# First 256 columns of x loaded as two times 128, with the first weight slab's rows between them, and the first feature tile multiplied ahead of the second's transposes

## The chip, the cores and the metric

The kernel runs on one core of a Trainium2 chip. The metric is device time in microseconds; the time of the kernel before is the median of three runs.

## The reference

One layer of a decoder trunk on x of 512 tokens by 2048 features, in float32:

```
h    = RMSNorm(x)
proj = h @ w_in                     # 2048 x 4608: q, k, v of two head groups
x    = x + concat(norm(stick_breaking(q, k, v)), norm(sliding_window(q, k, v))) @ w_out
h    = RMSNorm(x)
x    = x + (silu(gate) * up) @ w_down,   gate, up = split(h @ w_gate_up)
out  = RMSNorm(x)
```

The change lies in the first microseconds: the loading and transposing of x, and the first of the input projections, the values of the first head group (512 of w_in's columns at a time).

## The kernel before, in words

Every float32 product is done as three products of a cheaper format: an operand is split into a high part (rounded to fp32r by ScalarE, `hi`) and the rest (`lo`, by VectorE), and PE adds hi x hi, hi x lo and lo x hi in the same PSUM bank. So each operand costs one ScalarE and one VectorE instruction before PE can use it.

**The start.** x comes as four token tiles (128 tokens each) by column pieces `XC`, the first 256 columns wide. `load_x(0)` issues the four transfers of the first piece, `load(0)` two transfers of 128x512 of the first weight slab (one for each of its two rows of 128 features), `load_x(1)` the next four of x, `load(1)` slab 1 as one transfer of 512 KB. All go through SP's queue in program order (`dma` keeps it), and every transfer carries one of eight semaphores in turn, so that SP issues a transfer only when the one eight places ahead of it has landed. An issue can thus wait for a landing.

**Feature tiles.** `h_make(kt)` makes one feature tile of h: PE transposes the four token tiles' columns into a PSUM bank `z` (128 features by 512 tokens), ScalarE makes `hhi` of it, scaled by the norm's gain, VectorE `hlo` (`split_scaled`). The transposes are issued through `pT`, which pins them to program order; so are the matmuls of `warm(n)`, which multiply a constant `ones` into an unused bank, each showing as two instructions on PE. `split_scaled` itself is not pinned.

**Slabs.** A slab is 256 of the 2048 features of w_in by 512 columns; `queue` holds the slabs and, for each, 8 steps (`mms`): two feature tiles by four token tiles, three products each. `step()` does one: at a slab's step 0 it calls `split(i)` (if not done yet), at step 2 it loads the two slabs ahead and calls `split(i + 1)`, which for the first eight slabs first makes that slab's two feature tiles with `h_make`, then `whi` and `wlo` of the whole slab (128x1024). For slab 0 `split` goes by rows: `h_make(0)`, `whi` and `wlo` of row 0, then the same for row 1, with `pA` and `pV`, which pin. For later slabs they go through `A` and `V`, which do not. Where an instruction isn't pinned, the framework's scheduler places it in its engine's order when the program is built. The chip then runs each engine's list as it stands.

`x_squares` (row sums of squares of x for the norm, in place on ScalarE) are deferred to the last of these slabs in the program, and are put by the scheduler wherever ScalarE seems free.

Of the kernel before, what the change touches and what calls it, by code (L numbers as in the profile page):

```python
# [16 lines left out]
P = 128  # L17
# [20 lines left out]
def tile_hymba(ctx: ExitStack, tc: tile.TileContext, x, ln_mix, w_in, sb_norm, swa_norm,  # L38
               sinks, w_out, ln_ffn, w_gu, w_dn, ln_fin, out):
    nc = tc.nc  # L40
    x2d = x.rearrange("b s d -> (b s) d")
# [24 lines left out]
    def act8(name, dt=F32R):  # L66
        return act.tile([P, 4, 512], dt, tag="a8", name=name, bufs=8)
# [7 lines left out]
    def pz():  # L75
        return zs[1].tile([P, 512], F32, tag="z", name="z", bufs=4)
# [17 lines left out]
    def tmp(dt=F32, name="t"):  # L94
        return phase[1].tile([P, 512], dt, tag="t", name=name, bufs=phase[2])
# [3 lines left out]
    def dma(out, in_):  # L99
        tc.keep_in_program_order(nc.sync.dma_start(out=out, in_=in_))  # L100

    def f(ap):
        return ap.bitcast(F32)
# [49 lines left out]
    def warm(n):  # L153
        for _ in range(n):
            pT.matmul(busy[:, 0:P], lhsT=ones, rhs=ones, start=True, stop=True)
# [23 lines left out]
    def load(i):  # L179
        sl = queue[i]  # L180
        if "raw" in sl:
            return
        a, b, srcs = sl["a"], sl["b"], sl["srcs"]
        if sl["big"] is not None:

            if not sl["big"]:
                sl["big"].append(big_pool[0].tile([P, 2 * a, b], F32, tag="raw8", name="raw8", bufs=2))
                dma(out=sl["big"][0], in_=srcs[0].rearrange("(a p) c -> p a c", p=P))
                sl["raw"] = sl["big"][0][:, 0:a, :]
            else:  # L190
                sl["raw"] = sl["big"][0][:, a:2 * a, :]
            return
        raw = wp.tile([P, a, b], F32, tag="raw", name="raw", bufs=RAWB)
        n = b // len(srcs)
        if i == 0:
            for j in range(a):
                dma(out=raw[:, j, :], in_=srcs[0][j * P:(j + 1) * P, :])
            srcs = []
        for k, src in enumerate(srcs):
            dma(out=raw[:, :, k * n:(k + 1) * n], in_=src.rearrange("(a p) c -> p a c", p=P))  # L200
        sl["raw"] = raw

    def split(i):
        sl = queue[i]
        if "hi" in sl:
            return
        load(i)
        if sl["prep"] and i:
            sl["prep"]()
        a, b, raw = sl["a"], sl["b"], sl["raw"]  # L210
        hi = wp.tile([P, a, b], F32R, tag="whi", name="whi", bufs=2)
        lo = wp.tile([P, a, b], F32R, tag="wlo", name="wlo", bufs=2)
        if i == 0:
            for j in range(a):
                h_make(j)
                pA.activation(out=hi[:, j, :], in_=raw[:, j, :], func=AF.Copy)
                pV.tensor_tensor(out=lo[:, j, :], in0=raw[:, j, :], in1=f(hi)[:, j, :], op=ALU.subtract)
        else:
            A.activation(out=hi, in_=raw, func=AF.Copy)  # L219
            V.tensor_tensor(out=lo, in0=raw, in1=f(hi), op=ALU.subtract)  # L220
        sl["hi"], sl["lo"] = hi, lo
# [4 lines left out]
    def step():  # L226

        i, m = pos
        sl = queue[i]
        if m == 0:  # L230
            split(i)
            if sl["pre"]:
                sl["pre"]()
        if m == min(2, len(sl["mms"]) - 1):
            for k in (1, 2):
                if i + k < len(queue):
                    load(i + k)
            if i + 1 < len(queue):
                split(i + 1)
        t = sl["mms"][m](sl["hi"], sl["lo"])  # L240
        pos[1] += 1
        if pos[1] == len(sl["mms"]):
            pos[0] += 1
            pos[1] = 0
            if sl["post"]:
                sl["post"]()
        for d in list(due):
            d[0] -= 1
            if d[0] <= 0:
                due.remove(d)  # L250
                d[1]()
        return t

    def pull(ns, mark=None):

        mark = len(queue) if mark is None else mark
        carry[0] += ns
        while carry[0] > 0 and pos[0] < mark:
            carry[0] -= step()
# [4 lines left out]
    def drain(mark=None):  # L264

        mark = len(queue) if mark is None else mark
        while pos[0] < mark:
            step()

    def split_scaled(ps_ap, g_ap, hi, lo):  # L270
        A.activation(out=hi, in_=ps_ap, func=AF.Copy, scale=g_ap)
        V.scalar_tensor_tensor(out=lo, in0=ps_ap, scalar=g_ap, in1=f(hi), op0=ALU.mult, op1=ALU.subtract)
# [35 lines left out]
    XC = [(0, 256), (256, 256), (512, 512), (1024, 512), (1536, 512)]  # L308
    ss1 = const.tile([P, NT, len(XC)], F32, name="ss1")
    xs = {}  # L310
    rs1 = {}

    def load_x(c):
        c0, n = XC[c]
        for t in range(NT):
            xt = tmp(name="xt")[:, 0:n]
            dma(out=xt, in_=x2d[t * P:(t + 1) * P, c0:c0 + n])
            for k in range(n // P):
                xs[c0 // P + k, t] = xt[:, k * P:(k + 1) * P]
            xs["c", c, t] = xt  # L320

    def h_make(kt):
        pb = pz()
        for t in range(NT):
            pT.transpose(out=pb[:, t * P:(t + 1) * P], in_=xs[kt, t], identity=ident)
            warm({(0, 0): 1, (0, 1): 1, (0, 2): 3, (1, 3): 3}.get((kt, t), 0))
        if kt % 4 == 0:
            h8[0], h8[1] = act8("hhi"), act8("hlo")
        h_hi[kt], h_lo[kt] = h8[0][:, kt % 4, :], h8[1][:, kt % 4, :]
        split_scaled(pb, gcol[:, kt:kt + 1], h_hi[kt], h_lo[kt])  # L330
# [112 lines left out]
    def add_v(c):  # L443
        def v_done(t, pb):
            bv = pb.rearrange("p (h d) -> p h d", d=HD)
            split_scaled(bv, rs1["c"][:, t:t + 1], vst[t][:, c * 8:(c + 1) * 8, 0:HD],
                         vst[t][:, c * 8:(c + 1) * 8, HD:P])

        def prep(s):
            if c == 0:  # L450
                h_make(2 * s)
                h_make(2 * s + 1)
                if s == 7:
                    defer(1, lambda: [x_squares(k) for k in range(3)])
                    defer(2, lambda: [x_squares(k) for k in range(3, 5)])
                    defer(4, rstd1_make)
                    defer(8, rstd1_rows)
        add_tok(lambda s: win[s * 256:(s + 1) * 256, C_SBV + c * 512:C_SBV + (c + 1) * 512],
                8, 2, 512, hT, lambda: four(1 - c), v_done, prep)
# [11 lines left out]
    add_v(0)  # L471
    add_v(1)
    load_x(0)
    load(0)
    turn1()
    load_x(1)
    load(1)
    load_x(2)
    for c in (3, 4):
        while pos[0] < c - 3 or pos[1] < 3:  # L480
            step()
        load_x(c)
# [1176 lines left out]
```

## Time and profile before

| | us |
|---|---|
| median of 3 runs | 2019.59 (2019.31 to 2021.86) |
| the profiled execution's own time | 2019.78 |
| its span | 2017.7 |
| PE busy | 2004.0 |
| VectorE busy, ScalarE busy, GpSimd busy | 1454.5, 1455.9, 1030.7 |
| first product of the projection on PE (start) | 8.40 |
| first product of slab 1 on PE (start) | 14.95 |

The span is the stretch that the profiler saw, from the program's first instruction to its last; the time of an execution has 2.1 us around it. A row of the timeline gives start, length, engine, line, operation and tiles (out<-in, without numbers), the count of merged instructions, and in brackets the engine's idle time before it and what ended that. PE rows are pipelined: their lengths overlap, and start to start is what one costs. L118 is the line of the helper through which all pinned instructions go; L358 to L360 are there the three products of `one` in `add_tok`.

### The profile page before, as it was taken

The page shows a single profiled execution, that of the slowest core. Times are in us where ns is not written, and L with a number is a line of the kernel's source. Part 1 is how long each engine was busy: PE and PEld are TensorE (multiplying, and loading weights), DVE is VectorE, ACT ScalarE, POOL GpSimd, SP SyncE. Part 2 cuts the span into 40 slices and gives each one's busy share as a digit, 9 for nine tenths or more (in the row PEclk, how much of TensorE's full clock was granted, in tenths as well). Part 3 has the DMA queues.
Part 4 walks back from the last instruction along what each step waited for, and adds up shares of the span by engine and source line. Part 5 has one row for each costly group of instructions (what it writes and reads, how often), then busy time and mean ns, then how long its engine had stood idle before and what let it go on. Part 6 is the DMA issues. An engine that isn't in the chain of part 4 may idle for free.

```text
span 2017.7 us, 29248 instructions
## 1 busy us (share of the span) xinstructions
PE 2004.0 (99%) x10412; PEld 1708.3 (85%) x10412; DVE 1454.5 (72%) x1968; ACT 1455.9 (72%) x2009; POOL 1030.7 (51%) x562
## 2 busy tenths in 40 slices
PE   9999999999999999999999999999999999999998
PEld 8888888898888888888888888888888888888886
DVE  4358888778963777777777777777777867767767
ACT  5347777657842478777777777777777788788787
POOL 0014444300100066766666676666766778878883
PEclk9999999999999999999999999999999999999999
DMA  5322222222343354453544535444453743533523
GB/s 189 94 84 74 63 63 71 66 75 73 105 146 110 118 165 115 121 135 101 141 110 126 133 103 142 107 129 128 108 141 105 263 160 109 180 129 105 176 84 115
DMA packets 286369, 240.23 MB, mean 119 GB/s; under 512 B 11024, under 2 KB 237392, under 8 KB 283792
## 3 DMA queue, kind: packets, MB, share of 16 engines
q1 hardware_dynamic: 285552, 235.71, 39.5%
q8 instruction: 82, 1.34, 0.3%
q0 software_dynamic: 288, 1.32, 0.2%
q10 hardware_dynamic: 384, 1.34, 0.2%
q14 instruction: 63, 0.52, 0.1%
HBM read 218.40 MB, written 19.92 MB: 118 GB/s over the span
## 4 chain that ended last, share of the span: by engine, by line
PE 97%; DVE 1%; ACT 1%; issue 0%; DVEq 0%; POOL 0%; ACTq 0%; POOLq 0%
PE o L118 34%; PE m L118 28%; PE m L390 4%; PE m L391 4%; PE m L392 4%; PE m L359 2%; PE m L358 2%; PE m L360 2%; PE o L359 2%; PE o L360 2%; PE o L358 2%; PE z L118 1%; PE z L358 1%; PE z L359 1%; PE z L360 1%; PE o L685 1%
## 5 line engine op out<-in xcount | busy, mean ns | idle before, releaser
L118 POOL TENSOR_TENSOR t<-raw,t 128x1024 f32<-128x1024 f32 x107 | 272.6, 2548 | 278.0 <-ACT hp L118 263.7
L118 DVE TENSOR_TENSOR wlo<-t,hp 128x1024 fp32r<-128x1024 f32 x235 | 286.4, 1219 | 172.6 <-PE o L118 107.2
L118 ACT ACTIVATE whi<-t 128x1024 fp32r<-128x1024 f32 x235 | 249.2, 1061 | 123.7 <-PE o L118 75.3
L118 PE MATMUL o<-hca,whi 128*128 128x512 f32 x880 | 307.5, 391 | 0.0
L118 POOL TENSOR_TENSOR t<-raw,raw 128x1024 f32<-128x1024 f32 x106 | 275.1, 2599 | 16.6 <-issue 10.9
L118 DVE TENSOR_TENSOR wlo<-raw,hp 128x1024 fp32r<-128x1024 f32 x175 | 213.5, 1220 | 80.0 <-issue 49.8
L118 ACT ACTIVATE whi<-raw 128x1024 fp32r<-128x1024 f32 (+1 forms) x177 | 187.1, 1057 | 99.8 <-PE m L118 72.0
L118 PE MATMUL o<-hca,wlo 128*128 128x256 f32 x880 | 244.0, 280 | 0.0
L118 ACT ACTIVATE hp<-t 128x1024 fp32r<-128x1024 f32 x235 | 236.9, 1008 | 0.0
L220 DVE TENSOR_TENSOR wlo<-raw,whi 128x1024 fp32r<-128x1024 f32 x103 | 128.2, 1244 | 136.0 <-ACT whi L219 133.3
L219 ACT ACTIVATE whi<-raw 128x1024 fp32r<-128x1024 f32 x103 | 108.8, 1056 | 154.3 <-PE o L360 75.7
L118 PEld LDWEIGHTS o<-hca,whi 128*128 128x128 f32 x880 | 164.2, 187 | 35.8
L118 PE MATMUL m<-hca,whi 128*128 128x512 f32 x528 | 186.3, 392 | 1.1 <-DVE hca L118 1.1
L118 ACT ACTIVATE hp<-raw 128x1024 fp32r<-128x1024 f32 x179 | 180.8, 1010 | 3.3 <-DMA raw<-in_w_down_dram 1.8
L118 PEld LDWEIGHTS o<-hca,wlo 128*128 128x128 f32 x880 | 165.6, 189 | 0.4
L390 PE MATMUL m<-hhi,whi 128*128 128x512 f32 x384 | 156.3, 407 | 0.0
L391 PE MATMUL m<-hlo,whi 128*128 128x512 f32 x384 | 150.5, 392 | 0.0
L392 PE MATMUL m<-hhi,wlo 128*128 128x512 f32 x384 | 150.4, 392 | 0.0
L118 PE MATMUL m<-whi,dca 128*128 128x512 f32 x592 | 146.9, 389 | 0.0
L118 PE MATMUL o<-whi,dca 128*128 128x512 f32 x592 | 146.8, 389 | 0.0
L118 PE MATMUL m<-hca,wlo 128*128 128x256 f32 x528 | 146.3, 280 | 0.0
L118 PEld LDWEIGHTS o<-whi,dca 128*128 128x128 f32 x592 | 111.1, 188 | 23.0
(351 smaller groups left out, 5145.1 us busy)
## 6 DMA issues: line engine op xcount, KB each, us to landing
raw<-in_w_gate_up_dram SPq DMA_DIRECT2D x348, 256.0 KB, 5.2
raw<-in_w_down_dram SPq DMA_DIRECT2D x68, 512.0 KB, 4.9
raw<-in_w_in_dram SPq DMA_DIRECT2D x39, 512.0 KB, 3.6
raw<-in_w_in_dram SPq DMA_DIRECT2D x66, 256.0 KB, 3.3
raw<-in_w_out_dram SPq DMA_DIRECT2D x32, 512.0 KB, 3.8
aT<-w SPq DMA_DIRECT2D x44, 256.0 KB, 3.4
xd<-aT SPq DMA_DIRECT2D x10, 1024.0 KB, 6.8
rx<-in_w_down_dram SPq DMA_DIRECT2D x20, 512.0 KB, 5.6
```

Of the source, the lines that this page charges most:

```text
L118: return lambda *a, **k: tc.keep_in_program_order(fn(*a, **k))
L219: A.activation(out=hi, in_=raw, func=AF.Copy)
L220: V.tensor_tensor(out=lo, in0=raw, in1=f(hi), op=ALU.subtract)
L358: mm(o, lhsT=lh[:, sl], rhs=hi[:, j, :], start=first, stop=False, skip_group_check=halves)
L359: mm(o, lhsT=lh[:, sl], rhs=lo[:, j, :], start=False, stop=False, skip_group_check=halves)
L360: mm(o, lhsT=ll[:, sl], rhs=hi[:, j, :], start=False, stop=(k == nslab * a - 1), skip_group_check=halves)
L390: mm(o, lhsT=wh, rhs=xh, start=(k == 0), stop=False)
L391: mm(o, lhsT=wh, rhs=xl, start=False, stop=False)
L392: mm(o, lhsT=wl, rhs=xh, start=False, stop=(k == KT - 1))
L685: mm(H.ob[:, c0:S], lhsT=vb, rhs=B.wl[:, 0:W], start=False, stop=(i == 0), skip_group_check=True)
```

## The change

The first piece of x is no longer loaded by `load_x(0)`, which only notes tiles and sources in `x01`; `load(0)` issues four transfers of 128x128 (the first feature tile's columns), row 0 of slab 0, the other four of 128x128, and row 1. The second half of slab 0's preparation (`half(1)`: second feature tile, row 1's `whi` and `wlo`) moves from `split(0)` to slab 0's step 4, that is, behind the products of the first feature tile in program order, and `split(1)` from step 2 to step 5. The warm matmuls are set anew.

```
         if i == 0:
             for j in range(a):
+                for xt, src in x01:
+                    dma(out=xt[:, j * P:(j + 1) * P], in_=src[:, j * P:(j + 1) * P])
                 dma(out=raw[:, j, :], in_=srcs[0][j * P:(j + 1) * P, :])
...
-            for j in range(a):
+            def half(j):
                 h_make(j)
                 pA.activation(out=hi[:, j, :], in_=raw[:, j, :], func=AF.Copy)
                 pV.tensor_tensor(out=lo[:, j, :], in0=raw[:, j, :], in1=f(hi)[:, j, :], op=ALU.subtract)
+            half(0)
+            sl["half"] = half
...
+        if i == 0 and m == 4:
+            sl["half"](1)
         if m == min(2, len(sl["mms"]) - 1):
             for k in (1, 2):
                 if i + k < len(queue):
                     load(i + k)
+        if m == min(2 if i else 5, len(sl["mms"]) - 1):
             if i + 1 < len(queue):
                 split(i + 1)
...
-            dma(out=xt, in_=x2d[t * P:(t + 1) * P, c0:c0 + n])
+            src = x2d[t * P:(t + 1) * P, c0:c0 + n]
+            if c == 0:
+                x01.append((xt, src))
+            else:
+                dma(out=xt, in_=src)
...
-            warm({(0, 0): 1, (0, 1): 1, (0, 2): 3, (1, 3): 3}.get((kt, t), 0))
+            warm({(0, 0): 1, (0, 1): 1, (0, 2): 1, (0, 3): 3}.get((kt, t), 0))
```

The instructions change places in the first fifteen microseconds of the program; behind that, every engine's order is as before.

ScalarE at the program's start, before: `z_145` and `z_161` are the first and second feature tile, `raw_119` the first slab, `raw_133` slab 1, `z_185` and `z_192` the third and fourth tile.

```order
L271 ACTIVATE hhi_155<-z_145,gcol_97 128x512 [waits DVE_49,PE_49]
L118 ACTIVATE whi_143<-raw_119 128x512 [waits DMAHW5_49]
L271 ACTIVATE hhi_155<-z_161,gcol_97 128x512 [waits PE_49]
L118 ACTIVATE whi_143<-raw_119 128x512 [waits DMAHW6_49]
L219 ACTIVATE whi_199<-raw_133 128x1024 [waits DMAHW3_49]
L335 ACTIVATE xt_111,ss1_104<-xt_111 128x256 [waits DMAHW1_49]
L335 ACTIVATE xt_113,ss1_104<-xt_113 128x256 [waits DMAHW2_49]
L271 ACTIVATE hhi_155<-z_185,gcol_97 128x512 [waits PE_49]
```

ScalarE at the same place, now: `z_149` and `z_192` are the first and second feature tile, `raw_115` the first slab, `raw_137` slab 1, `z_204` the third tile.

```order
L279 ACTIVATE hhi_160<-z_149,gcol_97 128x512 [waits DVE_49,PE_49]
L118 ACTIVATE whi_147<-raw_115 128x512 [waits DMAHW5_49]
L224 ACTIVATE whi_218<-raw_137 128x1024 [waits DMAHW7_49]
L348 ACTIVATE xt_111,ss1_104<-xt_111 128x256 [waits DMAHW6_49,DMAHW1_49,PE_49]
L279 ACTIVATE hhi_160<-z_192,gcol_97 128x512 [waits PE_49]
L118 ACTIVATE whi_147<-raw_115 128x512 [waits DMAHW2_49]
L348 ACTIVATE xt_112,ss1_104<-xt_112 128x256
L348 ACTIVATE xt_113,ss1_104<-xt_113 128x256 [waits DMAHW3_49,DMAHW0_49]
L348 ACTIVATE xt_114,ss1_104<-xt_114 128x256 [waits DMAHW4_49,DMAHW1_49]
L279 ACTIVATE hhi_160<-z_204,gcol_97 128x512 [waits PE_49]
```

Slab 1's `whi`, with its wait for slab 1's transfer, moved from behind the second row's `whi` to a place ahead of the second tile's `hhi`. VectorE's `wlo` of slab 1 moved likewise, ahead of the second tile's `hlo`.

SP's transfers at the program's start, before:

```order
L100 DMA xt<-in_x_dram 128x256 x4
L100 DMA raw<-in_w_in_dram 128x512 x2
L100 DMA xt<-in_x_dram 128x256 x4
L100 DMA raw<-in_w_in_dram 128x2x512
L100 DMA xt<-in_x_dram 128x512 x4
```

SP's transfers at the same place, now:

```order
L100 DMA xt<-in_x_dram 128x128 x4
L100 DMA raw<-in_w_in_dram 128x512
L100 DMA xt<-in_x_dram 128x128 x4
L100 DMA raw<-in_w_in_dram 128x512
L100 DMA xt<-in_x_dram 128x256 x4
L100 DMA raw<-in_w_in_dram 128x2x512
L100 DMA xt<-in_x_dram 128x512 x4
```

Slab 1's transfer (the first 128x2x512) moved from the 11th place on SP to the 15th.

PE from the fourth token tile's transpose to the first products, before (`z_145` and `z_161` as above, `m_173` the first token tile's bank):

```order
L118 MATMUL z_145<-ident_85,xt_117 128x128 [waits DMAHW4_49]
L118 MATMUL z_161<-ident_85,xt_111 128x128
L118 MATMUL z_161<-ident_85,xt_113 128x128
L118 MATMUL z_161<-ident_85,xt_115 128x128
L118 MATMUL z_161<-ident_85,xt_117 128x128
L118 MATMUL o_98<-ones_90 128x128 x3
L358 MATMUL m_173<-whi_143,hhi_155 128x512 [waits Activation_49]
```

PE from the end of the first tile's products on, now (`m_166` to `o_169` are the four token tiles' banks):

```order
L372 MATMUL o_169<-wlo_148,hhi_160 128x512
L373 MATMUL o_169<-whi_147,hlo_161 128x512
L118 MATMUL z_192<-ident_85,xt_111 128x128 [waits DMAHW6_49]
L118 MATMUL z_192<-ident_85,xt_112 128x128 [waits DMAHW7_49]
L118 MATMUL z_192<-ident_85,xt_113 128x128 [waits DMAHW0_49]
L118 MATMUL z_192<-ident_85,xt_114 128x128 [waits DMAHW1_49]
L371 MATMUL m_166<-whi_147,hhi_160 128x512 [waits Activation_49]
L371 MATMUL m_167<-whi_147,hhi_160 128x512
```

The first two rows are the last of the first tile's 12 products; the second tile's transposes, which stood ahead of all products before, now stand behind them, and the row that waits for ScalarE is the first of the second tile's.

More of the change, by code (lines that the diff above doesn't have):

```diff
@@ L310, in tile_hymba @@
     xs = {}
+    x01 = []
     rs1 = {}
```

## The prediction

> **What bounds the kernel now.** I read the page first: TensorE (PE) is busy for 99% of the span, and it carries the chain that ended last.
>
> ```profile
> span 2017.7 us, 29248 instructions
> PE 2004.0 (99%) x10412; PEld 1708.3 (85%) x10412; DVE 1454.5 (72%) x1968; ACT 1455.9 (72%) x2009; POOL 1030.7 (51%) x562
> PE 97%; DVE 1%; ACT 1%; issue 0%; DVEq 0%; POOL 0%; ACTq 0%; POOLq 0%
> ```
>
> Then the waits of PE, over the whole span (total, times, longest, in us):
>
> ```profile
> PE o L118 <- POOL ones L127: 1.2, 1, 1.2
> PE m L118 <- DVE hca L118: 1.1, 1, 1.1
> PE o L685 <- DVE l L675: 0.4, 1, 0.4
> ```
>
> The first is the wait before PE's very first pass; after it nothing holds PE for more than 1.1 us, and the three largest together are 2.7 us. So nothing later can absorb a delay: if slab 1 starts late by some microseconds, the end is late by as much. The change touches only the first 15 us, so I read the timeline of that stretch, PE first (start, length, what):
>
> ```profile
> 1.21 2.50 PE L118 MATMUL o<-ones 128*128 128x128 f32 x10 [1.21 <-POOL ones L127]
> 5.40 1.49 PE L118 MATMUL o<-ones 128*128 128x128 f32 x6
> 6.68 0.92 PE L118 MATMUL z<-ident,xt 128*128 128x128 f32 x5
> 8.40 0.73 PE L358 MATMUL m<-whi,hhi 128*128 128x512 f32 x2
> 8.97 0.63 PE L358 MATMUL o<-whi,hhi 128*128 128x512 f32 x2
> 10.36 1.11 PE L118 MATMUL z<-ident,xt 128*128 128x128 f32 x8
> 11.22 0.48 PE L359 MATMUL o<-wlo,hhi 128*128 128x512 f32 x1
> 12.23 0.39 PE L358 MATMUL m<-whi,hhi 128*128 128x512 f32 x1
> 14.95 0.39 PE L358 MATMUL m<-whi,hhi 128*128 128x512 f32 x1
> 15.36 0.19 PEld L360 LDWEIGHTS m<-whi,hlo 128*128 128x128 f32 x1 [0.21 <-DVE hlo L272]
> ```
>
> PE idles on ready-made `ones` (warm) passes until the fourth token tile is transposed at 6.68. The real products run from 8.40, and slab 0 is done at 14.95 with its 24 products and the 8 transposes for slab 1 in between. Lengths overlap, so I count from start to start (a warm matmul is two rows, or passes): 12 products take 14.95 - 12.23 = 2.72 us (0.23 each), 8 transposes 11.22 - 10.36 = 0.86 us (0.11 each), the 6 warm passes 6.68 - 5.40 = 1.28 us (0.21 each). ScalarE (ACT) and VectorE feed it:
>
> ```profile
> 7.14 0.69 ACT L271 ACTIVATE hhi<-z,gcol 128x512 fp32r<-128x512 f32 x1 [5.05 <-PE z L118]
> 7.73 0.62 ACT L118 ACTIVATE whi<-raw 128x512 fp32r<-128x512 f32 x1
> 12.08 1.06 ACT L219 ACTIVATE whi<-raw 128x1024 fp32r<-128x1024 f32 x1 [2.64 <-DMA raw<-in_w_in_dram]
> 13.05 0.40 ACT L335 ACTIVATE xt<-xt 128x256 f32<-128x256 f32 x1
> 13.45 0.40 ACT L335 ACTIVATE xt<-xt 128x256 f32<-128x256 f32 x1
> 13.85 1.25 ACT L271 ACTIVATE hhi<-z,gcol 128x512 fp32r<-128x512 f32 x2
> ```
>
> The row at 12.08 matters most: it is slab 1's high half, and ACT stands idle for 2.64 us until slab 1's transfer has landed. ACT works in its order: the third feature tile was transposed by PE from 10.36, but its `hhi` ran only at 13.85, behind the waiting row and two squares. In the kernel before that costs nothing, since PE has slab 0's products until 14.95.
>
> **The change part by part.**
>
> *Earlier first products.* Between the third and fourth transpose two warm matmuls (four passes of 0.21) go: -0.85 us. From the fourth transpose to the first product it is 8.40 - 6.68 = 1.72 us, so the first product moves from 8.40 to 7.55, if the first half of the weights is there; it is still the fifth transfer on SP, with smaller ones ahead. PE then does the 12 products of the first feature tile (12 x 0.23 = 2.72, and 0.1 for the slower first) and the 4 transposes of the second (4 x 0.11 = 0.43): it is through at about 10.8.
>
> *The second half's place on ACT and VectorE.* Before, all of slab 0's preparation stood ahead of slab 1's. In the changed order slab 1's `whi` (and on VectorE its `wlo`) stands **between** the two halves: behind it on ACT are one square, then the second tile's `hhi` and the second row's `whi`. PE's 12 remaining products wait for those, and everything of PE stands behind. So PE is now bound to slab 1's landing. Call A the time at which ACT starts slab 1's `whi` (12.08 before). The durations from the rows above: to the square 13.05 - 12.08 = 0.97; the square 0.40 (13.45 to 13.85); `hhi` to `whi` 7.73 - 7.14 = 0.59; `whi` to the first product 8.40 - 7.73 = 0.67. PE resumes at A + 2.63. Then 12 products 2.72, a slower first one 0.11 (8.97 - 8.40 = 0.57 for two against 0.46), and slab 1's 8 transposes 0.86, which now stand in this half: slab 1's first product at A + 6.32. Before it was at 14.95, with 0.21 of a wait on `hlo` right behind it, which the changed order gives room: the third tile's transposes end 1.7 us earlier than that product. The shift is A + 6.32 - 15.16 = **A - 8.84**. PE's own early start drops out, because PE waits anyway.
>
> *When slab 1 lands.* SP's issues:
>
> ```profile
> 2.66 0.91 SPq L100 DMA_DIRECT2D raw<-in_w_in_dram  x2
> 3.61 1.86 SPq L100 DMA_DIRECT2D xt<-in_x_dram  x4
> 5.51 0.43 SPq L100 DMA_DIRECT2D raw<-in_w_in_dram  x1
> ```
>
> Four issues take 5.51 - 3.61 = 1.90 us, 0.475 each, whatever their size (the rows at 2.66 and 3.61 give the same for the 256 KB ones). Slab 1's transfer is the 11th of SP before and the 15th in the changed order, with the same bytes ahead (0.5 MB of x, 0.5 MB of weights, 0.5 MB of x): issued at 5.51 + 1.90 = 7.41 at the earliest. From issue to landing, the transfer at 5.51, a 512 KB one at 30.2 with nothing ahead of it, and the first of 128 KB:
>
> ```profile
> raw<-in_w_in_dram SPq DMA_DIRECT2D x1, 512.0 KB, 6.5
> raw<-in_w_in_dram SPq DMA_DIRECT2D x1, 512.0 KB, 3.6
> xt<-in_x_dram SPq DMA_DIRECT2D x1, 128.0 KB, 2.5
> 2.00:12.00 10.00, 9.87 (x53) 8.79 (x52) 2.79 (x5) 2.40 (x5) 1.03 (x4) 1.00 0.92 277
> ```
>
> The last row is the stretch from 2 to 12 us: the DMA engines are 0.92 busy and move 277 GB/s. Lower bound: 7.41 + 3.6 = 11.0, an empty queue, A = 11.05, shift +2.2. Upper bound: the issue delay is passed on in full, A = 12.08 + 1.90 = 13.98, shift +5.1. I take A = 12.1: of the 6.5 us before, 2.9 are queueing behind the same bytes, and a later issue shortens the queue by about what it costs. That is nearer to the empty queue's row plus half of the queueing (7.41 + 3.6 + 1.1) than to either end. Shift: 12.1 - 8.84 = **+3.3 us**. As a check by the stall: PE idle from 10.8 to 14.7 = 3.9, plus 0.11 restart, plus 0.43 for four transposes that lay ahead of 8.40 before, less 0.85 for the early start, less 0.21 = +3.4.
>
> *Edits at nothing.* The halves of x are 8 transfers of 64 KB in place of 4 of 128 KB; their cost is the issue time counted above. The second half's transposes wait for pieces issued by about 4.6, hidden by the first tile's products until 10.3; if that cover went, they would still be far ahead of slab 1's landing. Slab 3's transfer now waits for VectorE's later `wlo` of slab 0, about A + 3.6 = 15.7; it is needed only behind the products of slabs 1 and 2, 48 x 0.23 = 11 us on, and a transfer takes 3.6.
>
> *PE's pace after the stall.* At 5.40 a pass took 0.21 us, at 10.36 the same shape 0.11: the pace doubled at about 7, some 5.8 us after the first pass at 1.21. If a stall of 3.9 us puts PE back to the slow pace for as long, it loses half of 5.8, 2.9 us. No stall in mid-run is longer than 1.1 us, so the bounds are 0 and 2.9; I take 0, since nothing in the trace shows a way back to the slow pace, and keep 2.9 for the range. The Trainium skill ("TensorE: Matmul & The Clock Gate", Part 1 and "Why this matters for your kernels") has a rule that speaks against this change: one idle window of some 3.4 us puts the clock back to half, the windows run free of the program, and gaps over about 3 us are to be avoided. The doubling at 7 agrees with it; the way back no run here shows. By its figures the sum would be about +3.3 plus 1.7 to 3.4 wherever a stall covers a whole window, an estimate.
>
> **The rivals.** (1) *The slow pace comes back:* PE idle for 3.9 us runs at half pace for up to 5.8 us afterwards: +3.3 + 2.9 = +6.2, 2025.8 us. For it: the pace was low until 5.8 us of work; against: no stall of that length is in the trace. The skill's clock rule named above is this mechanism.
> (2) *Slab 1 lands late:* SP's delay is passed on whole, A = 13.98: +5.1, 2024.7. For it: at 2 to 12 us the engines are 0.92 busy and yet move only 277 GB/s, so some are held up, whatever is in the queue. Against: 1.9 us less queue.
> (3) *Not slower:* the hoisted row does no harm, because slab 1 is there before PE has used up the first half. This decides at A + 2.63 < 10.8, A below 8.2. Then PE's start counts: -0.85 + 0.43 (transposes that move behind it) - 0.21 = -0.6, 2019.0. Against it: the issue at 7.41 and even the quickest landing above, 2.5 us for a quarter of the bytes, give 9.9.
>
> **How the numbers follow.** The profiled execution took 2019.78 us, a span of 2017.7 and 2.1 around it, 0.2 above the median of 2019.59. The sum on the profiled execution is 2023.1; on the median **2022.9**. 0.2% of the time is 4.0 us, about what a measurement of this kernel can tell from no change, so the boundary lies at 2023.6. Chances: the forecast, A from 11.05 to 12.85 (+2.2 to +4.0), 0.53; rival 2, beyond that, 0.20; rival 1, 0.23; rival 3, 0.04. Within 0.2% are the forecast and rival 3, 0.56 with a little for noise; slower by more, 0.43; faster by more, 0.01. The range goes from the forecast's lower end less the spread of the runs (2021.8 - 0.3) to rival 1's time (2025.8 + 0.2): 2021.5 to 2026.0. The forecast's own range is 2021.8 to 2023.6.
>
> **What would show it.** Right: in the changed profile ACT waits for slab 1's transfer at about 8.2 to 12.1 with the second `hhi` right behind it; PE has one wait of about 3.9 us, ended by ACT, from 10.8; its first product is at about 7.5 and slab 1's first one at 18.4. SP issues slab 1 at about 7.4. Rival 1 shows as products 0.4 us apart after the wait; rival 2 as a landing after 12.9. Wrong: no wait of PE over 1 us near 11, a `hhi` of the second tile ahead of slab 1's `whi`, or a span that gets back what the first 20 us lost.

## The result, and the profile after

| | before | after |
|---|---|---|
| median of 6 runs, us | 2019.55 (2019.15 to 2021.86) | 2027.59 (2025.84 to 2028.19) |
| the profiled execution's time, its span | 2019.78, 2017.7 | 2028.19, 2026.1 |

The ratio is 1.0039, 95% interval 1.0029 to 1.0048: slower by 8.0 us, where 3.3 were predicted and 2026.0 was the end of the range. The profiled executions differ by 8.4 in span; the changed kernel's is the slowest of its six.

The page of the changed kernel, its span and busy times, shows the same work at nearly the same price (PE 2005.3 for 2004.0), in a span that is 8.4 longer:

```profile
span 2026.1 us, 29246 instructions
PE 2005.3 (99%) x10408; PEld 1708.8 (84%) x10408; DVE 1455.0 (72%) x1968; ACT 1456.4 (72%) x2009; POOL 1032.1 (51%) x562
```

The waits of PE (total, times, longest) have one new row, and it is the first; the two below it are the ones of before.

```profile
PE m L371 <- ACT whi L118: 7.1, 2, 6.5
PE o L118 <- POOL ones L127: 1.2, 1, 1.2
PE m L118 <- DVE hca L118: 1.1, 1, 1.1
```

PE's timeline says where it lies. L371 to L373 are the three products of `one`, L118 with `z<-ident,xt` the transposes.

```profile
7.08 0.73 PE L371 MATMUL m<-whi,hhi 128*128 128x512 f32 x2 [0.62 <-ACT whi L118]
9.96 0.60 PE L118 MATMUL z<-ident,xt 128*128 128x128 f32 x4
17.04 1.22 PE L371 MATMUL m<-whi,hhi 128*128 128x512 f32 x2 [6.48 <-ACT whi L118]
18.91 0.63 PE L372 MATMUL m<-wlo,hhi 128*128 128x512 f32 x1
19.34 0.63 PE L373 MATMUL m<-whi,hlo 128*128 128x512 f32 x1
19.76 1.91 PE L118 MATMUL z<-ident,xt 128*128 128x128 f32 x8
23.21 0.39 PE L371 MATMUL m<-whi,hhi 128*128 128x512 f32 x1
```

PE begins at 7.08, is through with the first feature tile and the second's transposes at 10.56 (9.96 + 0.60), and stands until 17.04. Then it works, but at half pace: a product each 0.43 us (18.91 to 19.34) instead of 0.23, a transpose each 0.2 instead of 0.11. Slab 1's first product, at 14.95 before, comes at 23.21: 8.26 later. Less the 0.21 that PE waited behind it before, that is 8.05 of the 8.4 by which the two profiled executions differ.

ACT's timeline shows what PE waited for:

```profile
6.41 0.62 ACT L118 ACTIVATE whi<-raw 128x512 fp32r<-128x512 f32 x1
14.44 1.06 ACT L224 ACTIVATE whi<-raw 128x1024 fp32r<-128x1024 f32 x1 [7.41 <-DMA raw<-in_w_in_dram]
15.40 0.40 ACT L348 ACTIVATE xt<-xt 128x256 f32<-128x256 f32 x1
15.80 0.67 ACT L279 ACTIVATE hhi<-z,gcol 128x512 fp32r<-128x512 f32 x1
16.37 0.62 ACT L118 ACTIVATE whi<-raw 128x512 fp32r<-128x512 f32 x1
```

The row at 14.44 answers to the one at 12.08 before. ACT has stood for 7.41 us until slab 1's transfer landed, and the second tile's `hhi` and the second row's `whi`, whose data have long been there, stand behind it, with a square between. So A is 14.44, and PE resumes at A + 2.60.

SP's issues around slab 1's transfer, in the changed kernel:

```profile
5.03 0.43 SPq L100 DMA_DIRECT2D raw<-in_w_in_dram  x1
5.50 1.85 SPq L100 DMA_DIRECT2D xt<-in_x_dram  x4
7.40 0.43 SPq L100 DMA_DIRECT2D raw<-in_w_in_dram  x1
```

Slab 1 is issued at 7.40, as worked out (7.41), and 7.0 us later ACT has it; before, the landing took 6.5.

The stretches of PE (length, PE busy and instructions, granted clock, DMA share, GB/s) show why it ran slowly:

```profile
14.00:15.00 1.00, 0.00 (x0) 1.00 1.05 402
15.00:16.00 1.00, 0.00 (x0) 0.70 1.05 406
16.00:17.00 1.00, 0.00 (x0) 0.50 1.07 408
21.00:22.00 1.00, 1.00 (x6) 0.50 1.02 356
22.00:23.00 1.00, 1.00 (x6) 0.88 1.04 381
```

The granted clock is 0.70 in the stretch from 15 to 16: 1.00 for 0.4 us and 0.50 for the rest. So it fell at 15.4, while PE still waited, and it came back at 22.24 (0.88 is 0.24 us at half and the rest at full clock), after 6.8 us. In the views of before it is 1.00 all along. (The views show 1.00 for the first microseconds of every trace too, in which a pass takes 0.21 us instead of 0.11: a trace's clock record begins only where that pace doubles, at 7.11 in the kernel before and at 5.17 in the changed one.) The wait is thus followed by a second loss: 23.21 - 17.04 = 6.17 us for the 12 products and 8 transposes, which at full clock take 3.86 (the experiments below).

### The profile page after: what moved, and what is told of

It is laid out like the page before. It is cut to its first block, busy times and chain, and to the rows that moved or that the text cites. A ratio compares the mean times of both kernels' runs of the same rounds, so it can differ in the third digit from the quotient of the medians.

```text
span 2026.1 us, 29246 instructions
## 1 busy us (share of the span) xinstructions
PE 2005.3 (99%) x10408; PEld 1708.8 (84%) x10408; DVE 1455.0 (72%) x1968; ACT 1456.4 (72%) x2009; POOL 1032.1 (51%) x562
## 4 chain that ended last, share of the span: by engine, by line
PE 96%; DVE 1%; ACT 1%; DMA 0%; SPq 0%; issue 0%; DVEq 0%; ACTq 0%
PE o L118 34%; PE m L118 28%; PE m L403 4%; PE m L404 4%; PE m L405 4%; PE m L372 2%; PE m L371 2%; PE m L373 2%; PE o L371 2%; PE o L373 2%; PE o L372 2%; PE z L118 1%; PE z L371 1%; PE z L372 1%; PE z L373 1%; PE z L866 1%
## 5 line engine op out<-in xcount | busy, mean ns | idle before, releaser
L118 POOL TENSOR_TENSOR t<-raw,t 128x1024 f32<-128x1024 f32 x107 | 272.6, 2547 | 277.5 <-ACT hp L118 263.4
L118 DVE TENSOR_TENSOR wlo<-t,hp 128x1024 fp32r<-128x1024 f32 x235 | 286.5, 1219 | 172.4 <-PE o L118 108.3
L118 ACT ACTIVATE whi<-t 128x1024 fp32r<-128x1024 f32 x235 | 249.3, 1061 | 123.6 <-PE o L118 75.2
L118 PE MATMUL o<-hca,whi 128*128 128x512 f32 x880 | 307.5, 391 | 0.0
L118 POOL TENSOR_TENSOR t<-raw,raw 128x1024 f32<-128x1024 f32 x106 | 275.3, 2600 | 16.3 <-issue 11.8
L118 DVE TENSOR_TENSOR wlo<-raw,hp 128x1024 fp32r<-128x1024 f32 x175 | 213.6, 1221 | 80.0 <-issue 50.6
L118 ACT ACTIVATE whi<-raw 128x1024 fp32r<-128x1024 f32 (+1 forms) x177 | 187.1, 1057 | 99.9 <-PE m L118 72.1
L118 PE MATMUL o<-hca,wlo 128*128 128x256 f32 x880 | 244.0, 280 | 0.0
L118 ACT ACTIVATE hp<-t 128x1024 fp32r<-128x1024 f32 x235 | 236.9, 1008 | 0.3 <-POOL t L118 0.3
L118 PEld LDWEIGHTS o<-hca,whi 128*128 128x128 f32 x880 | 164.2, 187 | 35.8
L118 PE MATMUL m<-hca,whi 128*128 128x512 f32 x528 | 186.3, 392 | 1.1 <-DVE hca L118 1.1
L118 ACT ACTIVATE hp<-raw 128x1024 fp32r<-128x1024 f32 x179 | 180.8, 1010 | 3.4 <-DMA raw<-in_w_down_dram 2.4
L118 PEld LDWEIGHTS o<-hca,wlo 128*128 128x128 f32 x880 | 165.6, 189 | 0.4
L118 PE MATMUL m<-whi,dca 128*128 128x512 f32 x592 | 146.9, 389 | 0.0
L118 PE MATMUL o<-whi,dca 128*128 128x512 f32 x592 | 146.9, 389 | 0.0
L118 PE MATMUL m<-hca,wlo 128*128 128x256 f32 x528 | 146.3, 280 | 0.0
L118 PEld LDWEIGHTS o<-whi,dca 128*128 128x128 f32 x592 | 111.1, 188 | 23.1
```

Source lines behind the costliest of these rows:

```text
L118: return lambda *a, **k: tc.keep_in_program_order(fn(*a, **k))
```

## The experiments

Two parts of the change were under suspicion, the loads and the order, and two mechanisms, the late landing and the pace. Each kernel is timed against the kernel before on the same chip; the before of the first four has a median of 2019.48, that of the next three 2019.62.

**Order fixed.** The changed kernel, with slab 1's split pinned, so that the scheduler can't move it ahead of the second half:

```
-            A.activation(out=hi, in_=raw, func=AF.Copy)
-            V.tensor_tensor(out=lo, in0=raw, in1=f(hi), op=ALU.subtract)
+            (pA if i == 1 else A).activation(out=hi, in_=raw, func=AF.Copy)
+            (pV if i == 1 else V).tensor_tensor(out=lo, in0=raw, in1=f(hi), op=ALU.subtract)
```

> The changed kernel with slab 1's high and low halves pinned to program order, so that on ScalarE and VectorE they stand behind the second feature tile and the second row again; loads and the order on PE's first half as in the changed kernel. Theory (the hoisted row binds PE to slab 1's landing, and the idle PE falls to half pace): PE's wait of 6.5 us near 10.6 shrinks to some 1.5 us, the products stay 0.23 us apart, slab 1's first product comes at about 16 us instead of 23.2 (slab 1 still lands at about 14.4, and its low half is ready 2.3 us later), so the time is about 1 to 2 us above the kernel before, 2020.5 to 2021.5. Rival (the eight small transfers hold the engines up whatever the order on ScalarE): the time stays within 1.5 us of the changed kernel, 2026 to 2028.

Measured: 2022.30 (2021.74 to 2022.41, 11 runs), ratio 1.0013 [1.0005, 1.0022], 5.3 us below the changed kernel. The clock in its trace is 1.00. So two thirds of the loss belong to the hoisted row, with all that followed from it, the late pace included. The rest, 2.8, is more than expected. ACT and PE of this kernel, and slab 1's transfer (median us from issue to landing, issued at 7.41):

```profile
11.74 0.62 ACT L118 ACTIVATE whi<-raw 128x512 fp32r<-128x512 f32 x1
14.55 1.27 ACT L279 ACTIVATE hhi<-z,gcol 128x512 fp32r<-128x512 f32 x2 [0.99 <-PE z L118]
15.71 1.06 ACT L118 ACTIVATE whi<-raw 128x1024 fp32r<-128x1024 f32 x1
```

```profile
12.41 0.73 PE L371 MATMUL m<-whi,hhi 128*128 128x512 f32 x2 [1.36 <-ACT whi L118]
16.82 0.73 PE L371 MATMUL m<-whi,hhi 128*128 128x512 f32 x2 [0.48 <-ACT whi L118]
```

```profile
raw<-in_w_in_dram SPq DMA_DIRECT2D x1, 512.0 KB, 6.5
```

Slab 1 landed at 13.9, but its `whi`, pinned, now stood behind the third and fourth tile's `hhi` and ran at 15.71; and the second half, made only after the first tile's products, cost a wait of 1.36 at 12.41. Those two waits, not the transfer, held PE here.

**Loads alone.** The kernel before, in its own order, with the halves of x and the first weights between them:

```
         if i == 0:
             for j in range(a):
+                for xt, src in x01:
+                    dma(out=xt[:, j * P:(j + 1) * P], in_=src[:, j * P:(j + 1) * P])
                 dma(out=raw[:, j, :], in_=srcs[0][j * P:(j + 1) * P, :])
...
-            dma(out=xt, in_=x2d[t * P:(t + 1) * P, c0:c0 + n])
+            src = x2d[t * P:(t + 1) * P, c0:c0 + n]
+            if c == 0:
+                x01.append((xt, src))
+            else:
+                dma(out=xt, in_=src)
```

> The kernel before with the changed loads alone: the first piece of x in two times 128 columns, each with its weight row behind; both feature tiles ahead of all products, and the warm matmuls of before. Theory: no hoisted row, so PE has slab 0's products until 14 to 15 us; slab 1 still lands at about 14.4 (SP's 15th place), its feature tiles stand behind its high half on ScalarE, and its first product comes at about 17: 2 to 2.5 us above the kernel before, 2021.5 to 2022, no slow pace. Rival (small transfers cost by themselves what the change lost): 2026 to 2028. Third way (slab 1's landing depends on when PE and ScalarE run, not on SP's place): it lands at about 12 as before, and the time is that of before.

Measured: 2021.65 (2021.21 to 2022.39, 11 runs), ratio 1.0011 [1.0002, 1.0019], 2.2 above. ACT's row of slab 1, and PE's wait for x:

```profile
13.18 1.06 ACT L221 ACTIVATE whi<-raw 128x1024 fp32r<-128x1024 f32 x1 [3.96 <-DMA raw<-in_w_in_dram]
```

```profile
PE z L118 <- DMA xt<-in_x_dram: 1.2, 2, 0.8
```

Slab 1 is 1.1 later than before, PE waits twice for x, and the clock stays at 1.00. The time is the expected one, but not by the expected way: slab 1 landed at 13.2 and not at 14.4, and its first product came at 15.78 and not at 17, 0.83 later than before. Slab 2's came 1.11 later (22.47 for 21.36), while the profiled execution is 1.6 longer in span; where the rest is lost is open.

**Order alone.** The changed kernel with the first piece of x loaded as before:

```
-                for xt, src in x01:
-                    dma(out=xt[:, j * P:(j + 1) * P], in_=src[:, j * P:(j + 1) * P])
...
-            if c == 0:
-                x01.append((xt, src))
-            else:
-                dma(out=xt, in_=src)
+            dma(out=xt, in_=src)
```

> The changed kernel with the loads of the kernel before: the hoisted row is there, but slab 1 is SP's 11th transfer again. Theory: slab 1 lands at about 12.1, PE waits from 10.7 to 14.7, about 4 us, and slab 1's first product comes at 18.4 if the pace holds and up to 20.9 if it falls: 3.3 us above the kernel before (2022.8), or 5 to 6 where the pace falls. Rival (the loads alone make the loss): the time of before within 1 us.

Measured: 2023.52 (2022.08 to 2024.25, 11 runs), ratio 1.0019 [1.0010, 1.0028], 4.0 above. ACT's row of slab 1, PE's restart and slab 1's first product, and the stretches of PE:

```profile
10.65 1.06 ACT L222 ACTIVATE whi<-raw 128x1024 fp32r<-128x1024 f32 x1 [2.73 <-DMA raw<-in_w_in_dram]
```

```profile
13.25 0.73 PE L366 MATMUL m<-whi,hhi 128*128 128x512 f32 x2 [1.82 <-ACT whi L118]
18.73 0.39 PE L366 MATMUL m<-whi,hhi 128*128 128x512 f32 x1
```

```profile
14.00:15.00 1.00, 1.00 (x4) 0.71 1.05 399
17.00:18.00 1.00, 1.00 (x4) 0.58 1.06 410
```

Back at the 11th place on SP, slab 1 comes in time for a short wait. Yet a wait of 1.82 us was enough for the clock to fall, from 14.42 to 17.84, which I had not thought of.

**PE kept busy in the wait.** The changed kernel with 24 constant matmuls behind the second tile's transposes:

```
+        if kt == 1:
+            wz = pz()
+            for _ in range(24):
+                pT.matmul(wz[:, 0:P], lhsT=ones, rhs=ones, start=True, stop=True)
```

> The changed kernel with 24 warm matmuls of the constant (48 passes, 5.3 us at the quick pace) behind the second feature tile's transposes, into a bank of their own, so that PE works through most of the wait; nothing else is earlier. Theory (half pace after the wait costs about 2.5 us): ScalarE ends the wait at about 17 as before, the products then run 0.23 us apart, and the time is 1.5 to 2.5 us below the changed kernel, 2025 to 2026. Rival (the pace is nothing, the wait all): the changed kernel's time, 2027.5, within 0.5.

Measured: 2026.19 (2025.35 to 2026.67, 6 runs), ratio 1.0032 [1.0020, 1.0044]: 1.4 below the changed kernel, just short of what was expected. In its trace the clock is 1.00 all along and the products stand 0.23 apart, but `wlo` of the second row holds PE for 0.53, since PE no longer takes twice as long for the products ahead of it. From A (13.59) to slab 1's first product (20.73) it is 7.14, against 8.77 in the changed kernel: 1.6 us, the pace won back less the wait for `wlo`. Slab 1 also came 0.85 earlier in this execution (13.59 for 14.44), so how much of the 1.4 between the medians is pace, the times alone don't tell.

**Slab 1 issued early.** The changed kernel with small pieces and all, but slab 1 ahead of the next piece of x, at SP's 11th place again:

```
-    load_x(1)
     load(1)
+    load_x(1)
```

> The changed kernel with slab 1's transfer issued ahead of the second piece of x: SP's 11th place instead of the 15th, small pieces and the hoisted row kept. Theory (PE is bound one to one to slab 1's landing, and the landing follows SP's place): slab 1 is issued 1.9 us earlier and lands at 11 to 12.5 instead of 14.4, and the time falls by 2 to 3 us against the changed kernel, to 2024.5 to 2025.5 with the slow pace still there. Rival (the small pieces make it late, not the place): it lands at 13.5 to 14.5 and the time stays at 2027 to 2028.

Measured: 2022.41 (2021.28 to 2024.01, 11 runs), ratio 1.0015 [1.0006, 1.0024], 5.2 below the changed kernel and more of a gain than expected. ACT's row of slab 1, PE's restart and slab 1's first product:

```profile
10.35 1.06 ACT L224 ACTIVATE whi<-raw 128x1024 fp32r<-128x1024 f32 x1 [3.42 <-DMA raw<-in_w_in_dram]
```

```profile
12.95 0.73 PE L371 MATMUL m<-whi,hhi 128*128 128x512 f32 x2 [2.50 <-ACT whi L118]
16.80 0.39 PE L371 MATMUL m<-whi,hhi 128*128 128x512 f32 x1
```

The small pieces of x are all ahead of slab 1 here, and it landed by 10.35. So the small pieces alone don't make it late. With its place, the second piece of x (0.5 MB) has gone behind it as well; that alone isn't the reason either, since in the order alone all 1.5 MB are ahead of slab 1, at the 11th place, and A was 10.65. What is common to the late landings is the 15th place, 1.9 us later, behind small pieces and the second piece of x; no run separates these further. And 2.50 us of waiting, more than in the order alone, left the clock at 1.00.

**Order alone, PE kept busy.** The order alone with nine of the constant matmuls:

```
+        if kt == 1:
+            wz = pz()
+            for _ in range(9):
+                pT.matmul(wz[:, 0:P], lhsT=ones, rhs=ones, start=True, stop=True)
```

> The order-only kernel (hoisted row, loads of before) with 9 warm matmuls behind the second tile's transposes, 18 passes, 2 us, which fill its wait of 1.8 us. Theory (a wait of under 2 us is enough for the slow pace, which cost that kernel's profile 1.8 us): no product 0.43 us apart after 13 us, and 2021.7 to 2022.3 instead of 2023.5. Rival (the slow pace in that profile was chance, and the median has little of it): 2023 to 2024.

Measured: 2022.96 (2022.06 to 2025.19, 11 runs), ratio 1.0018 [1.0010, 1.0027]: 0.56 below the order alone, less than expected, and with spreads that overlap (2022.08 to 2024.25 there) not to be told from nothing. It lies at the edge of what the rival said. The clock stayed at 1.00 in its profile and `wlo` held PE for 0.53. I had counted the slow pace as if every execution of the order alone had it.

**The same two kernels again.** The times of the order alone and of slab 1 issued early are spread over 2 to 3 us (of order fixed, over 0.7), and seem to lie in two groups each. Both were profiled twice more, to see whether the clock falls in some executions and not in others.

> The same kernel as e3_order_only (order alone), looked at again with a profile. Its eleven times lie in two groups, 2022.1 to 2022.9 (four) and 2023.4 to 2024.3 (seven); in its profile the granted clock was 0.50 from about 14.4 to 17.8 us after a wait of 1.82 us. Theory (the clock goes by windows of 3.4 us that stand differently to the program in each execution): the profile of an execution of the upper group shows the clock at 0.50 for about 3.4 us soon after the wait, one of the lower group shows 1.00 throughout, with the wait as long as before (1.5 to 2.5 us) in both. Rival (the length of the wait decides, and with it slab 1's landing): the clock falls whenever the wait is over about 1.8 us, and the two groups are late and early landings.

> As for e3_second_look: the same kernel once more. Theory: a fall, if there is one, begins at another distance from the wait's end, lasts 3.4 us, and goes with a time of 2023.4 or more; without a fall the time is below 2023. Rival: the fall goes with the wait's length.

> The same kernel as e5_slab1_early, looked at again with a profile. Its times lie in 2021.3 to 2022.4 (seven) and 2023.1 to 2024.0 (four); its profile showed a wait of 2.50 us and a granted clock of 1.00 throughout. Theory: an execution of the upper group shows the clock at 0.50 for about 3.4 us after the wait, one of the lower group none, with waits alike. Rival: no fall after a wait of about 2.5 us in any execution of this kernel, and the groups are late and early landings.

> As for e5_second_look: the same kernel once more. Theory: in about four of eleven executions a fall of 3.4 us, with a time of 2023 or more; otherwise none. Rival: none in any.

Measured: the order alone 2023.04 and 2021.73, slab 1 issued early 2022.04 and 2023.08. PE's restart and slab 1's first product, in the third profile of the order alone, then in the second and in the third of slab 1 issued early:

```profile
13.03 0.74 PE L366 MATMUL m<-whi,hhi 128*128 128x512 f32 x2 [1.67 <-ACT whi L118]
16.89 0.39 PE L366 MATMUL m<-whi,hhi 128*128 128x512 f32 x1
```

```profile
13.30 0.73 PE L371 MATMUL m<-whi,hhi 128*128 128x512 f32 x2 [2.75 <-ACT whi L118]
17.16 0.39 PE L371 MATMUL m<-whi,hhi 128*128 128x512 f32 x1
```

```profile
12.90 1.11 PE L371 MATMUL m<-whi,hhi 128*128 128x512 f32 x2 [1.88 <-ACT whi L118]
18.25 0.39 PE L371 MATMUL m<-whi,hhi 128*128 128x512 f32 x1
```

| execution | wait, us | pace doubles at the start | clock at 0.50 in the first 30 us | restart to slab 1's first product | time |
|---|---|---|---|---|---|
| order alone, first | 1.82 | 7.59 | 14.42 to 17.84 | 5.48 | 2023.44 |
| order alone, second | 1.85 | 6.57 | 13.40 to 16.80 | 5.35 | 2023.04 |
| order alone, third | 1.67 | 6.91 | never | 3.86 | 2021.73 |
| slab 1 early, first | 2.50 | 4.96 | never | 3.85 | 2022.44 |
| slab 1 early, second | 2.75 | 5.15 | never | 3.86 | 2022.04 |
| slab 1 early, third | 1.88 | 6.23 | 13.06 to 16.47 | 5.35 | 2023.08 |

The same kernel shows a fall after 1.88 us and none after 2.75. So the length of the wait alone does not decide, and the rival falls. Each fall lasts 3.4 us, begins 0.2 to 1.2 us after the restart, when PE is busy again, and costs 1.5 to 1.6 us.

Windows of 3.41 us that stand differently to the program each time account for all six, and the traces show where these windows stand. The third column is the time at which the passes at the program's start go from 0.21 to 0.11 us, where the trace's clock record begins. Each fall lies two windows behind it: 7.59 + 6.83 = 14.42, 6.57 + 6.83 = 13.40, 6.23 + 6.83 = 13.06; in the changed kernel it is three, 5.17 + 10.24 = 15.41. These are the windows that hold the wait (length, PE busy and instructions, granted clock, DMA share, GB/s), of the order alone, first and third, then the two of slab 1 early, second, and the one of slab 1 early, third, with the one behind it:

```profile
11.01:14.42 3.41, 1.59 (x9) 1.00 1.03 374
10.32:13.73 3.41, 1.74 (x10) 1.00 1.03 368
8.56:11.97 3.41, 1.98 (x11) 1.00 1.06 367
11.97:15.39 3.42, 2.09 (x11) 1.00 0.92 327
9.64:13.06 3.42, 1.54 (x10) 1.00 1.05 366
13.06:16.47 3.41, 3.41 (x11) 0.50 1.06 387
```

Ahead of the three falls PE stands idle for 1.82 to 1.88 us of one window, 53 to 55% of it; in the third profile of the order alone it is 1.67, 49%, and the clock stays. The waits of 2.50 and 2.75 are cut in two by a window's end (at 11.78 and 11.97), and no part is over 42% of its window. In the changed kernel the window from 11.99 to 15.40 is idle as a whole; the next is busy for 1.78 of 3.42, and the clock came back only behind the one after that, in which PE was busy throughout. So in the first 30 us of all the traces the clock, once up, fell behind the windows of which PE was idle for 53% or more, and behind none with 49% or less. That half of a window is the exact limit isn't shown: at the end of the program, in the second profile of the order alone, a window idle for 55% (1.54 of 3.41 busy) was not followed by a fall.

The clock isn't the whole spread. With PE kept busy, the order alone's times lie over 3.1 us, and the one of them that was profiled took 2023.08 with the clock at 1.00; A was 11.05 there, against 10.25 to 10.65 without the constant matmuls. A time of 2023.4 for a fall, as expected, was too high by 0.4.

**The best order.** The order alone, with the second half at step 1 instead of step 4 (its transposes stand behind six products in the trace) and slab 1's split pinned ahead of the third and fourth tile:

```
-        if i == 0 and m == 4:
+        if i == 0 and m == 1:
             sl["half"](1)
...
-        if sl["prep"] and i:
+        if sl["prep"] and i > 1:
             sl["prep"]()
...
-            A.activation(out=hi, in_=raw, func=AF.Copy)
-            V.tensor_tensor(out=lo, in0=raw, in1=f(hi), op=ALU.subtract)
+            (pA if i == 1 else A).activation(out=hi, in_=raw, func=AF.Copy)
+            (pV if i == 1 else V).tensor_tensor(out=lo, in0=raw, in1=f(hi), op=ALU.subtract)
+            if i == 1:
+                sl["prep"]()
```

> The loads of before, the change's fewer warm matmuls and its first products ahead of the second tile's transposes, but these already at step 1 (so that ScalarE makes the second tile while PE multiplies the first), slab 1's halves pinned behind both and ahead of the third tile's. Theory (all that the change can win is the earlier first product, as soon as no row waits out of turn): no wait of PE over 0.5 us, slab 1's first product at 14.2 to 14.8 instead of 14.95, 0.3 to 0.9 us below the kernel before, 2018.6 to 2019.2. Rival (slab 1's landing at 12 with its tiles behind it is the bound anyway): that of before, 2019.5, within 0.2.

Measured: 2019.95 (2019.41 to 2020.31, 11 runs), ratio 1.0003 [0.9994, 1.0012]: the whole loss is gone, and there is no gain. The third tile's `hhi`, and slab 1's first products:

```profile
13.90 1.24 ACT L279 ACTIVATE hhi<-z,gcol 128x512 fp32r<-128x512 f32 x2
```

```profile
14.65 0.47 PE L368 MATMUL m<-whi,hhi 128*128 128x512 f32 x1
15.41 0.50 PE L370 MATMUL m<-whi,hlo 128*128 128x512 f32 x1
```

Slab 1 starts 0.3 earlier than before, but its third product, the first to need the third tile's `hlo`, runs at 15.41, just as 0.21 of waiting put it before: ACT does three squares ahead of that tile's `hhi`.

**Tiles ahead of squares.** The best order with those splits pinned ahead of the first squares, against a before of 2019.61:

```
-        A.activation(out=hi, in_=ps_ap, func=AF.Copy, scale=g_ap)
+        (pA if pin else A).activation(out=hi, in_=ps_ap, func=AF.Copy, scale=g_ap)
...
-        split_scaled(pb, gcol[:, kt:kt + 1], h_hi[kt], h_lo[kt])
+        split_scaled(pb, gcol[:, kt:kt + 1], h_hi[kt], h_lo[kt], kt < 4)
...
-            A.activation(out=xt, in_=xt, func=AF.Square, accum_out=ss1[:, t, c:c + 1])
+            (pA if c == 0 else A).activation(out=xt, in_=xt, func=AF.Square, accum_out=ss1[:, t, c:c + 1])
...
+                if s == 1:
+                    x_squares(0)
...
```

> e6_best_order with the splits of the third and fourth tile pinned ahead of the first squares on ScalarE. In e6_best_order slab 1's third product waited until 15.41, as in the kernel before, for a hlo whose hhi stood behind three squares at 13.90. Theory (that split is what binds once slab 1's place is kept): the third tile's hhi now runs about 0.97 after slab 1's whi starts (at about 12.7), slab 1's third product follows its first two without a gap (0.46 behind the first, at about 15.1 or earlier), and the time is 0.3 to 0.7 us below e6_best_order's 2019.95, that is 2019.3 to 2019.7: at the kernel before or a few tenths below, hardly to be told from it. Rival (something else binds there, such as slab 1's wlo on VectorE or slab 2's landing): the gap at the third product stays or moves to slab 2, and the time is that of e6_best_order.

Measured: 2019.48 (2019.26 to 2019.90, 11 runs), ratio 1.0000 [0.9991, 1.0009].

```profile
13.16 1.27 ACT L118 ACTIVATE hhi<-z,gcol 128x512 fp32r<-128x512 f32 x2 [1.10 <-PE z L118]
```

```profile
14.79 0.39 PE L368 MATMUL m<-whi,hhi 128*128 128x512 f32 x1
15.25 0.39 PE L370 MATMUL m<-whi,hlo 128*128 128x512 f32 x1
```

The third product follows at 0.46 from the first, and slab 2 starts at 21.14 instead of 21.36. So that split was what bound, but with it gone the early start is worth 0.2 us, which no time here can tell from nothing.

## Why the prediction was wrong

**Right: the mechanism.** The hoisted row made PE wait for slab 1's landing, and PE's own early start dropped out: it began at 7.08, 0.47 earlier than worked out, for nothing. (Its pace at the start doubled at 5.17, by the windows above; with the order fixed, the same program up to there, it doubled at 7.25 and the first product came at 7.55 as worked out.) SP's issue came at 7.40 for 7.41, PE's restart at A + 2.60 for A + 2.63. The 12 products and 8 transposes behind it take 3.86 at full clock, 0.17 more than the sum had. With the order fixed, 5.3 of the 8.0 us are gone; with the loads of before as well, in the best order, all of it.

**Wrong: the landing.** The step was "I take A = 12.1 ... a later issue shortens the queue by about what it costs". A was 14.44, above the upper bound of 13.98. It goes with the slab's place on SP: A was 10.3 to 12.1 in nine executions of five kernels with slab 1 at the 11th place (the kernel before, with 12.08, is the latest of them); with slab 1 at the 15th, A was 13.2, 13.6 and 14.4, and with the order fixed slab 1 landed at 13.9. The means, 10.8 and 13.8, are 2.9 apart, for an issue 1.9 later. So the runs show nothing saved in the queue, and the bound, worked out from one execution, left out that A differs by 1.8 us among those nine. Why the delay is passed on with more on top isn't settled; the small pieces alone are not the reason, since slab 1 landed early behind them. This term is 2.3 us of the 4.7 that were missing (14.44 - 12.1).

**Wrong: the pace.** The step was "I take 0, since nothing in the trace shows a way back to the slow pace". The clock fell to 0.50 for 6.8 us, and the same work took 6.17 instead of 3.86: 2.3 us, inside the bound of 2.9. That bound took the 5.8 us up to the doubling at the start for the length of the slow pace; in the other traces the doubling came 3.7 to 6.4 us after the first pass (4.95 to 7.59, less 1.21), so 5.8 was one draw. Where PE was kept busy in the wait, the clock stayed up and the time was 1.4 us lower. The Trainium skill ("TensorE: Matmul & The Clock Gate", Part 1) has free-running windows of about 3.4 us, and a fall after at least one idle window. The length agrees (falls of 3.42, 3.40 and 3.41, and twice that, 6.8, in the changed kernel), and so does the free run (the table above); in the changed kernel a whole window was idle, from 11.99 to 15.40, and the fall came at its end. That a window has to be idle, and the Trainium skill's advice to avoid gaps over about 3 us ("Why this matters for your kernels"), differ from the traces: waits of 1.82, 1.85 and 1.88, 53 to 55% of a window, were followed by a fall. The measurement decides.

**The rivals** were priced one at a time, the slow pace at 2025.8 and the late landing at 2024.7. They are not alternatives: the later the landing, the longer the wait and the surer the fall. Added, +5.1 and +2.9, they give 2027.6, a case that stood nowhere in the chances and that the range did not reach. That this is the measured time is in part luck: the landing was 0.5 later than its bound, and the slow pace cost 0.6 less than its own. Rival 3 had the landing against it, and rightly. Of the 8.4 us between the profiled executions 8.2 were there when slab 2 began (29.54 for 21.36), and nothing gave them back.

## What to carry to other kernels

An instruction that isn't pinned may be placed ahead of others that are ready, and then its transfer holds the engine that is the bottleneck: look at the list of each engine, not at the program, before a stage is split. Four more transfers ahead of a large one on a queue put it back here by 1.9 us in its issue and by 2.9 in its landing, by the means of the runs. Rivals that share a cause are to be priced together as well as apart, and a wait of PE from about 1.8 us on, just over half of a window of 3.41, is to be priced with its clock.

## What the runs showed of the hardware

- The granted clock changed only at steps of 3.41 us, counted from the doubling of the pace at the start, which came between 4.95 and 7.59 us. In the first 30 us it fell behind a window of which PE was idle for 53% or more, and not behind one with 49% or less. So in the two kernels that were profiled three times it fell only once PE was busy again, and not after the longest waits.
- Slab 1's 512 KB took 4.7 to 7.0 us from issue until ACT had it (the second profile of the order alone, and the changed kernel), against 3.6 to the landing for such a transfer at 30.2 in the kernel before. From 2 to 12 us the changed kernel's DMA engines were 0.82 busy and moved 215 GB/s, less than before (0.92 and 277); from 14 to 15 us they moved 402. From 8 to 13 us, while slab 1 is on its way, it was 230 to 277 GB/s in the four kernels that have it at SP's 15th place, and 317 to 368 in the ten executions that have it at the 11th. Why it is less isn't settled.

```profile
2.00:12.00 10.00, 7.93 (x42) 6.66 (x40) 1.52 (x3) 1.29 (x3) 1.02 (x4) 1.00 0.82 215
```
